# One low-part subtraction for each weight tile of a two-layer hybrid decoder

## The chip, the cores and the metric

The kernel runs on one core of one Trainium2 chip, in one launch. The metric is the device time in microseconds (us); a measurement is the median of several runs. The span named below is that of one execution taken by the profiler, from its first instruction to its last.

## The reference, cut to what matters

Two layers of a decoder on 256 tokens of width 1024, all in float32. Each layer has a token mixer, a cross attention to 256 memory tokens, and a feed-forward part: a dense SwiGLU in layer 0 and eight experts in layer 1, of which each token takes two.

```python
def swiglu(h, w_gate, w_up, w_down):
    a = jnp.einsum("bsd,df->bsf", h, w_gate)
    u = jnp.einsum("bsd,df->bsf", h, w_up)
    return jnp.einsum("bsf,fd->bsd", jax.nn.silu(a) * u, w_down)

def moe_swiglu(h, router_w, w_gate, w_up, w_down):
    ...
    for e in range(N_EXPERTS):
        y = y + gates[..., e:e + 1] * swiglu(h, w_gate[e], w_up[e], w_down[e]).astype(jnp.float32)

def reference(x, mem, ...):
    for l in range(DEPTH):
        x = x + hybrid_mixer(rmsnorm(x, norm_mix_w[l]), w_in[l], ...)
        x = x + memory_cross_attention(...)
        h = rmsnorm(x, norm_ffn_w[l])
        x = x + (swiglu(h, ...) if l % 2 == 0 else moe_swiglu(h, ...))
    return rmsnorm(x, norm_final_w)
```

The weights of the eight experts (D = 1024, width 2816) are three quarters of all bytes.

## The kernel before

**Weight tiles.** All weights come in tiles of 128 x 2048 float32 (1 MB), in the order of `weight_order`. A tile is loaded by SyncE into a staging buffer (`wst` or `wsp`). TensorE multiplies in the format fp32r; to keep float32 precision each operand is split into a high part and a low part. ScalarE makes the high part of a tile (`wh`, a rounding copy), VectorE the low part (`wl` = staged - `wh`). A product then takes three matmuls (`mm3`): high x low, low x high, high x high. When the low part is made, the staging buffer is free and SyncE, which waits for that, loads another tile.

**Buffers of the parts.** `Halves` keeps each part in two buffers of 1024 columns. Five such halves lie in a ring for `wh` and five for `wl`; in the expert stage there are seven for `wh` and six for `wl`.

**Trunk and expert stage.** Up to the dense layer and the second mixer ("trunk" below) Tile's scheduler sets the order of instructions, and `halve` splits tiles with low parts of 512 columns. The expert stage (from about 585 us) has its order written out by hand: `slot` stands for one weight tile, 264 in all, and the engines execute what it lists in that order. In slot t ScalarE makes the high halves of tile t+2, VectorE the low halves of tile t+1, TensorE the products of tile t. Small steps of the expert's own chain are posted to a later slot, at a place within it: `"act"` ahead of the first high half, `"act mid"` between the two, `"dve mid"` between the two low halves, `"pe mid"` between the two halves of the products, `"pe"` behind them.

**Long and short experts.** Experts are sorted by their number of tokens. A *long* one has up to 128 tokens: gate-up tile 12 matmuls, down tile 12. A *short* one has up to 64: its tokens' high and low parts stand side by side in the 128 columns, so a tile takes 8 matmuls, first the one with `wl`, then the one with `wh`, for each of four pieces. A chunk is 256 of the 2816 hidden channels: two gate-up tiles (`eg`) and, a few slots later, one down tile (`ed`). From the seventh long chunk on, long and short chunks come in turn, so a period of six slots is: long gate-up, long gate-up, long down (of the chunk before), short gate-up, short gate-up, short down. There are 44 chunks of each kind; the last short ones have no long one beside them.

**The chain of a chunk.** Long: ScalarE's SiLU (`es`), VectorE's product (`es`), two transposes on TensorE at the end of the next slot (`et`), ScalarE's high copy (`ehh`), VectorE's low part (`ehl`). Short: ScalarE copies the sums (`eg`), TensorE turns and adds them with eight small matmuls (`et`) in the middle of the next slot, ScalarE's SiLU, VectorE's product, then the two parts (`ehh` from both engines).

The first matmuls of a short down tile, and where they take their operands:

```python
def down(ps, h, n, k, start, stop, wh, wl):
    fs = slice(k * 1024 + n * 512, k * 1024 + (n + 1) * 512)
    for w in (wl, wh):
        nc.tensor.matmul(ps[n], h[:, k], w[:, fs], ...)
```

`products[0]` is n = 0 with k = 0 and then k = 1: two matmuls on the first half of the tile (`wl`, `wh`), then two on the second half.

Of the kernel before, what the change touches and what calls it, by code (L numbers as in the profile page):

```python
# [2 lines left out]

# [4 lines left out]
F32 = mybir.dt.float32  # L8
F32R = mybir.dt.float32r
# [3 lines left out]
ALU = mybir.AluOpType  # L13
# [3 lines left out]
P = 128  # L17
T = 256
NT = T // P
D = 1024  # L20
KD = D // P
# [12 lines left out]
LEAD = 1  # L34
CUT = (512, 1024)
STAGES = (4, 1)
HALVES = (5, {"wh": 2, "wl": 1})
WARM = (40, 72, 30, 14)
URGENT = 500
C = 64  # L40
# [43 lines left out]

class Norm:
    pass


class Halves:


    def __init__(self, *tiles):
        self.tiles = tiles

    def __getitem__(self, at):
        p, s = at
        h = s.start // 1024
        return self.tiles[h][p, s.start - h * 1024:s.stop - h * 1024]


class Trunk:
# [77 lines left out]
        self.fetched = self.nc.sync.dma_start(dst, src)  # L179
        return slot, st  # L180

    def halves(self, name):
        return Halves(*[next(self.pools[name]).tile([P, 1024], F32R, name=name) for _ in range(2)])

    def halve(self, slot, st):

        nc, tc = self.nc, self.tc
        wh, wl = self.halves("wh"), self.halves("wl")
        for q in range(2):
            s = slice(q * 1024, (q + 1) * 1024)  # L190
            self.halved = nc.scalar.activation(wh[:, s], st[:, s], AF.Copy)  # L191
            for c in range(0, 1024, self.cut):
                s = slice(q * 1024 + c, q * 1024 + c + self.cut)
                with tc.issue_after(self.hold.ins) if self.hold else nullcontext():
                    nc.vector.tensor_tensor(wl[:, s], st[:, s], wh[:, s].bitcast(F32), op=ALU.subtract)  # L195
        self.free.append(slot)
        return wh, wl
# [38 lines left out]
    def high(self, i, q):  # L236

        if i >= len(self.order) or i < self.nsplit:
            return
        if q == 0:  # L240
            self.stage()
            self.parts[i] = *self.loaded.pop(0), self.halves("wh"), self.halves("wl")
        _, st, wh, _ = self.parts[i]
        s = slice(q * 1024, (q + 1) * 1024)
        self.nc.scalar.activation(wh[:, s], st[:, s], AF.Copy)  # L245

    def low(self, i, q):
        if i not in self.parts:
            return
        slot, st, wh, wl = self.parts[i]  # L250
        s = slice(q * 1024, (q + 1) * 1024)
        with self.tc.issue_after(self.hold.ins) if self.hold else nullcontext():
            self.nc.vector.tensor_tensor(wl[:, s], st[:, s], wh[:, s].bitcast(F32), op=ALU.subtract)  # L253
        if q == 1:
            self.hold = None
            self.ready[self.order[i][0]] = wh, wl
            del self.parts[i]
            self.free.append(slot)
            self.stage()

    def slot(self, key, *products):
        t = self.nused
        assert self.order[t][0] == key, (self.order[t][0], key)
        self.now += 1
        if t + 1 < len(self.order) and t + 1 >= self.nsplit and t + 1 not in self.parts:
            self.high(t + 1, 0)
            self.high(t + 1, 1)
        self.places("act")
        self.high(t + 2, 0)
        self.low(t + 1, 0)  # L270
        self.places("dve mid", "act mid")
        self.high(t + 2, 1)
        self.low(t + 1, 1)
        w = self.ready.pop(key)
        products[0](*w)
        self.places("pe mid")
        products[1](*w)
        self.places("pe")
        self.nused += 1

    def rest(self):

        self.now += 1
        self.places("act", "dve mid", "act mid", "pe mid", "pe")


    def build(self):
# [3 lines left out]
        self.wst = pool("wst", STAGES[0])  # L291
        slot = lambda p: lambda: p.tile([P, 2048], F32, name="wst")
        self.free = [slot(self.wst)] * STAGES[0]
        self.wp = pool("wp", HALVES[0])
        self.pools = {n: repeat(self.wp) for n in ("wh", "wl")}
        self.ps = pool("ps", 8, space=PSUM)
        self.sm = pool("sm", 4)
        self.t8 = pool("t8", 6)
# [72 lines left out]
                if l % 2 == 0:  # L371
                    self.dense(l // 2, l)
        with tc.tile_pool(name="emid", bufs=1) as self.md, tc.tile_pool(name="ewkb", bufs=2) as self.wb, \
                tc.tile_pool(name="wst2", bufs=STAGES[1]) as wst2, ExitStack() as more:
            self.free += [slot(wst2)] * STAGES[1]
            for n, k in HALVES[1].items():
                p = more.enter_context(tc.tile_pool(name=f"{n}2", bufs=k))
                self.pools[n] = cycle([p] * k + [self.wp] * HALVES[0])
            self.xg = [self.big("xg", shape=(P, 2 * KD * P)) for _ in range(2)]
            self.spare()  # L380
            self.kept = self.spare()
            self.moe(0, 1)
# [818 lines left out]
    def moe(self, j, l):  # L1201
# [22 lines left out]
        def gather(lists, xg):  # L1224
# [10 lines left out]
            ps = {}  # L1235
# [35 lines left out]
            def spread(n):  # L1271

                for k in range(KD):
                    self.post(n + k, "pe", lambda k=k: products(k))
                    self.post(n + k + 1, "act mid", lambda k=k: highs(k))
                    self.post(n + k + 2, "dve mid", lambda k=k: lows(k))
                self.post(n + KD, "pe", scales)
                self.post(n + KD + 1, "dve mid", keep_scales)

            return xg, xr, steps, spread  # L1280

# [85 lines left out]
        def long(x, xr):  # L1367
            def part(pg, hf, k, wh, wl):
                c = hf * 4 + k
                fs = slice(k * 512, (k + 1) * 512)  # L1370
                self.mm3(pg, x[:, c, 0], x[:, c, 1], wh[:, fs], wl[:, fs], c == 0, c == KD - 1)

            def chain(pg):

                s = wb.tile([P, 256], F32, name="es")
                h = [wb.tile([P, 2, P], F32R, name=f"eh{p}", bufs=3) for p in "hl"]
                pt = self.psum((P, 2, P), "et")

                def turn():
                    for k in range(2):  # L1380
                        nc.tensor.transpose(pt[:, k, :], s[:, k * P:(k + 1) * P], self.ident)

                self.post(1, "act", lambda: nc.scalar.activation(s, pg[:, 0:256], AF.Silu, scale=xr))
                self.post(1, "dve mid", lambda: nc.vector.scalar_tensor_tensor(
                    s, pg[:, 256:512], xr, s, op0=ALU.mult, op1=ALU.mult))
                self.post(1, "pe", turn)
                self.post(2, "act", lambda: self.split_hi(h[0], pt))
                self.post(2, "dve mid", lambda: self.split_lo(*h, pt))
                return h

            def down(ps, h, n, k, start, stop, wh, wl):
                fs = slice(k * 1024 + n * 512, k * 1024 + (n + 1) * 512)
                self.mm3(ps[n], h[0][:, k, :], h[1][:, k, :], wh[:, fs], wl[:, fs], start, stop)

            return part, chain, down

        def short(x, xr):
# [13 lines left out]
            def chain(pg):  # L1411
# [10 lines left out]
                self.post(1, "act", lambda: nc.scalar.activation(g, pg, AF.Copy))  # L1422
                self.post(1, "pe mid", turn)
                self.post(2, "act", lambda: nc.scalar.activation(s, pt[:, 0:2, :], AF.Silu))
                self.post(2, "dve mid", lambda: nc.vector.tensor_tensor(s, s, pt[:, 2:4, :], op=ALU.mult))
                self.post(2, "act mid", lambda: self.split_hi(hs[:, :, 0, :], s))
                self.post(3, "dve mid", lambda: self.split_lo(hs[:, :, 0, :], hs[:, :, 1, :], s))
                return h

            def down(ps, h, n, k, start, stop, wh, wl):  # L1430
# [6 lines left out]
        def leave(ps, oh, gate):  # L1437
# [17 lines left out]
            rows()  # L1455
            for n in range(2):
                self.post(1 + n, "act", lambda n=n: self.split_hi(y[n][0], ps[n]))
                self.post(1 + n, "dve mid", lambda n=n: self.split_lo(*y[n], ps[n]))
            self.post(1, "dve mid", lambda: nc.vector.tensor_copy(oT, po[:, 0:T]))
            for n in range(2):  # L1460
                for i in range(NT):
                    pz = self.psum(name="ez")
                    self.post(2 + 2 * n + i, "pe", lambda pz=pz, i=i, n=n: scatter(pz, i, n))
                    self.post(3 + 2 * n + i, "dve mid", lambda pz=pz, i=i, n=n: add(pz, i, n))

        class Expert:

# [55 lines left out]
        def spread(n):  # L1523
            marks, _, rest = lists_of(n)
            for i, m in enumerate(marks):
                self.post(1 + i, "dve mid", m)
            rest(1 + len(marks))

        with self.urgent():
# [81 lines left out]
    def final_weights(self):  # L1611

        nc = self.nc
# [8 lines left out]

        for k in range(8):
            b = k // 4
            self.post(1 + k, "dve mid", lambda k=k: diagonal(k))
# [97 lines left out]
```

## Time and profile before

| what | value |
|---|---|
| median of 3 runs (lowest to highest) | 1342.04 us (1341.5 to 1342.77) |
| the profiled execution's own time | 1343.5 us |
| its span | 1341.6 us |
| mean granted TensorE clock | 0.990 |
| TensorE busy | 1293.9 us, 96% of the span |
| VectorE busy | 1162.9 us, 87% |
| ScalarE busy | 937.6 us, 70% |
| read from HBM | 365.60 MB, 273 GB/s over the span |

A busy share is an average over stages: the trunk (to about 585 us) and the expert stage have different limits. In the profile PE is TensorE's matmuls, PEld its weight loads, DVE is VectorE, ACT ScalarE, SP SyncE; L253 is line 253 of the kernel.

### The profile page before, as it was taken

What the parts mean: (1) busy time and instruction counts of PE and PEld (TensorE: products, weight loads), DVE (VectorE), ACT (ScalarE), POOL (GpSimd) and SP (SyncE); (2) the same over time, 40 slices, a digit from 0 to 9 for tenths busy, and PEclk for the clock granted to TensorE, in tenths of its full rate; (3) what the DMA queues carried; (4) which work ended last, traced back from release to release, by engine and by line L of the source; (5) the groups of instructions that cost most, each with busy time, mean ns of one, the idle gap of its engine ahead of it and who ended that gap; (6) DMA issues with size and microseconds to landing.
All of it is one profiled execution on the core that took longest, in us unless ns stands there. A gap on an engine that the chain in (4) does not pass through costs nothing.

```text
span 1341.6 us, 20691 instructions
## 1 busy us (share of the span) xinstructions
PE 1293.9 (96%) x7301; PEld 1087.7 (81%) x7301; DVE 1162.9 (87%) x2057; ACT 937.6 (70%) x1502; POOL 7.5 (1%) x30
## 2 busy tenths in 40 slices
PE   9999999999999999989999999999999999999995
PEld 8978989999999878778877787777877778777773
DVE  8998877666677988579999999999999999999997
ACT  7565575444465556558788788887888887887884
POOL 0000000000000000000000000000000000000000
PEclk9999999999999999979999999999999999999998
DMA  8423625555544424549999999999999999999990
GB/s 326 158 96 118 228 95 194 187 187 189 187 165 151 164 95 160 194 149 338 343 405 386 338 371 413 379 402 338 355 412 384 394 380 337 404 407 371 392 351 34
DMA packets 67567, 368.06 MB, mean 274 GB/s; under 512 B 5744, under 2 KB 6000, under 8 KB 38016
## 3 DMA queue, kind: packets, MB, share of 16 engines
q1 hardware_dynamic: 67136, 365.59, 72.1%
q8 instruction: 59, 0.97, 0.3%
q0 software_dynamic: 320, 1.08, 0.2%
q14 instruction: 52, 0.43, 0.1%
HBM read 365.60 MB, written 1.05 MB: 273 GB/s over the span
## 4 chain that ended last, share of the span: by engine, by line
PE 68%; DVE 20%; issue 7%; ACT 5%; DMA 0%; DVEq 0%; SPq 0%; ACTq 0%
DVE wl L253 12%; PE fm L437 5%; PE fm L439 5%; PE fm L438 5%; PE eg L437 5%; PE eg L439 5%; PE eg L438 5%; PE ed L1433 4%; PE ed L437 2%; PE ed L438 2%; PE ed L439 2%; PE et L1420 2%; PE pr L437 2%; PE pr L438 2%; PE pr L439 2%
## 5 line engine op out<-in xcount | busy, mean ns | idle before, releaser
L253 DVE TENSOR_TENSOR wl<-wst,wh 128x1024 fp32r<-128x1024 f32 x294 | 348.9, 1222 | 0.0
L245 ACT ACTIVATE wh<-wst 128x1024 fp32r<-128x1024 f32 x294 | 295.6, 1053 | 0.0
L195 DVE TENSOR_TENSOR wl<-wst,wh 128x512 fp32r<-128x512 f32 x328 | 214.8, 688 | 87.9 <-ACT wh L191 87.7
L253 DVE TENSOR_TENSOR wl<-wsp,wh 128x1024 fp32r<-128x1024 f32 x232 | 276.1, 1222 | 1.5 <-PE eg L438 1.5
L191 ACT ACTIVATE wh<-wst 128x1024 fp32r<-128x1024 f32 x164 | 171.3, 1062 | 143.7 <-PE fm L439 88.5
L245 ACT ACTIVATE wh<-wsp 128x1024 fp32r<-128x1024 f32 x232 | 234.4, 1054 | 0.3 <-PE eg L439 0.3
L437 PE MATMUL fm<-hTh,wl 128*128 128x256 f32 x736 | 207.6, 282 | 1.0 <-DVE wl L195 1.0
L438 PE MATMUL fm<-hTl,wh 128*128 128x256 f32 x736 | 206.2, 280 | 0.0
L439 PE MATMUL fm<-hTh,wh 128*128 128x256 f32 x736 | 205.9, 280 | 0.0
L1409 PE MATMUL eg<-wl,xs 128*128 128x512 f32 x352 | 143.9, 409 | 5.9 <-DVE wl L253 5.9
L437 PE MATMUL eg<-wh,xg 128*128 128x512 f32 x352 | 141.2, 401 | 0.0
L437 PEld LDWEIGHTS fm<-hTh,wl 128*128 128x128 f32 x736 | 138.3, 188 | 1.9 <-DVE wl L195 1.2
L438 PE MATMUL eg<-wl,xg 128*128 128x512 f32 x352 | 139.8, 397 | 0.0
L439 PE MATMUL eg<-wh,xg 128*128 128x512 f32 x352 | 139.8, 397 | 0.0
L438 PEld LDWEIGHTS fm<-hTl,wh 128*128 128x128 f32 x736 | 138.2, 188 | 0.8 <-issue 0.2
L439 PEld LDWEIGHTS fm<-hTh,wh 128*128 128x128 f32 x736 | 138.7, 188 | 0.0
L1409 PE MATMUL eg<-wh,xs 128*128 128x512 f32 x352 | 138.6, 394 | 0.0
L1433 PE MATMUL ed<-wl,ehh 128*128 128x512 f32 x176 | 78.1, 444 | 13.5 <-DVE wl L253 12.2
L1409 PEld LDWEIGHTS eg<-wl,xs 128*128 128x128 f32 x352 | 66.3, 188 | 23.4 <-DVE wl L253 10.7
L439 PEld LDWEIGHTS eg<-wh,xg 128*128 128x128 f32 x352 | 66.8, 190 | 15.7
L437 PEld LDWEIGHTS eg<-wh,xg 128*128 128x128 f32 x352 | 67.0, 190 | 14.8
L438 PEld LDWEIGHTS eg<-wl,xg 128*128 128x128 f32 x352 | 66.9, 190 | 14.8
(339 smaller groups left out, 2257.0 us busy)
## 6 DMA issues: line engine op xcount, KB each, us to landing
wst<-in_moe_gu_dram SPq DMA_DIRECT2D x115, 1024.0 KB, 7.0
wsp<-in_moe_gu_dram SPq DMA_DIRECT2D x61, 1024.0 KB, 6.9
wsp<-in_moe_w_down_dram SPq DMA_DIRECT2D x55, 1024.0 KB, 7.2
wst<-in_moe_w_down_dram SPq DMA_DIRECT2D x33, 1024.0 KB, 7.3
wst<-in_ffn_gu_dram SPq DMA_DIRECT2D x22, 1024.0 KB, 4.9
wst<-in_w_in_fm_dram SPq DMA_DIRECT2D x16, 1024.0 KB, 4.9
wst<-in_ffn_w_down_dram SPq DMA_DIRECT2D x11, 1024.0 KB, 4.9
wst<-in_w_in_tm_dram SPq DMA_DIRECT2D x8, 1024.0 KB, 5.0
```

Of the source, the lines that this page charges most:

```text
L191: self.halved = nc.scalar.activation(wh[:, s], st[:, s], AF.Copy)
L195: nc.vector.tensor_tensor(wl[:, s], st[:, s], wh[:, s].bitcast(F32), op=ALU.subtract)
L245: self.nc.scalar.activation(wh[:, s], st[:, s], AF.Copy)
L253: self.nc.vector.tensor_tensor(wl[:, s], st[:, s], wh[:, s].bitcast(F32), op=ALU.subtract)
L437: nc.tensor.matmul(out, ll, rh, start=start, stop=False)
L438: nc.tensor.matmul(out, lh, rl, start=False, stop=False)
L439: nc.tensor.matmul(out, lh, rh, start=False, stop=stop)
L1409: nc.tensor.matmul(pg, both[:, c], w[:, fs], start=c == 0 and w is wl, stop=c == KD - 1 and w is wh)
L1420: nc.tensor.matmul(pt[:, b, :], g[:, b * P:(b + 1) * P], comb, start=True, stop=True)
L1433: nc.tensor.matmul(ps[n], h[:, k], w[:, fs], start=start and w is wl, stop=stop and w is wh)
```

## The change

- `Halves` is gone. A part is one buffer of 128 x 2048, three for `wh` and three for `wl`, from the start to the end of the kernel. A high part is still written by two instructions of 1024 columns.
- In the expert stage `low` makes the whole low part of tile t+1 in one instruction of 2048 columns. What was posted between two low halves (`"dve mid"`) now stands behind it (`"dve"`).
- ScalarE's high part of a short chunk's hidden values goes from slot 2, `"act mid"`, to slot 3, `"act"`.
- In the trunk `halve` still works in pieces of 512 columns, but its pieces lie in whole buffers.

```diff
-HALVES = (5, {"wh": 2, "wl": 1})
+SPLITS = {"wh": 3, "wl": 3}
...
+    def parts_of(self):
+        return [self.wp.tile([P, 2048], F32R, name=n, bufs=SPLITS[n]) for n in ("wh", "wl")]
...
-            self.parts[i] = *self.loaded.pop(0), self.halves("wh"), self.halves("wl")
+            self.parts[i] = *self.loaded.pop(0), *self.parts_of()
...
-    def low(self, i, q):
+    def low(self, i):
         if i not in self.parts:
             return
-        slot, st, wh, wl = self.parts[i]
-        s = slice(q * 1024, (q + 1) * 1024)
+        slot, st, wh, wl = self.parts.pop(i)
         with self.tc.issue_after(self.hold.ins) if self.hold else nullcontext():
-            self.nc.vector.tensor_tensor(wl[:, s], st[:, s], wh[:, s].bitcast(F32), op=ALU.subtract)
-        if q == 1:
-            self.hold = None
-            self.ready[self.order[i][0]] = wh, wl
-            del self.parts[i]
-            self.free.append(slot)
-            self.stage()
+            self.nc.vector.tensor_tensor(wl, st, wh.bitcast(F32), op=ALU.subtract)
+        self.hold = None
+        self.ready[self.order[i][0]] = wh, wl
+        self.free.append(slot)
+        self.stage()
...
         self.places("act")
         self.high(t + 2, 0)
-        self.low(t + 1, 0)
-        self.places("dve mid", "act mid")
+        self.low(t + 1)
+        self.places("dve", "act mid")
         self.high(t + 2, 1)
-        self.low(t + 1, 1)
...
-                self.post(2, "act mid", lambda: self.split_hi(hs[:, :, 0, :], s))
-                self.post(3, "dve mid", lambda: self.split_lo(hs[:, :, 0, :], hs[:, :, 1, :], s))
+                self.post(3, "act", lambda: self.split_hi(hs[:, :, 0, :], s))
+                self.post(3, "dve", lambda: self.split_lo(hs[:, :, 0, :], hs[:, :, 1, :], s))
```

All other `"dve mid"` posts become `"dve"` alike. On VectorE, in a period in which long and short chunks come in turn, these rows stood before (from a long chunk's product `es` on; `wl_9111` and `wl_9112` are the halves of the first short gate-up tile, `wl_9139` and `wl_9140` of the second, `wl_9166` and `wl_9167` of the short down tile):

```order
L253 TENSOR_TENSOR wl_9111<-wst_8928,wh_9109 128x1024
L1384 SCALAR_TENSOR_TENSOR es_9132<-eg_9083,xr2_7094,es_9132 128x256
L253 TENSOR_TENSOR wl_9112<-wst_8928,wh_9110 128x1024
L253 TENSOR_TENSOR wl_9139<-wsp_6681,wh_9137 128x1024
L451 TENSOR_TENSOR ehl_9134<-et_9135,ehh_9133 128x256
L253 TENSOR_TENSOR wl_9140<-wsp_6681,wh_9138 128x1024
L253 TENSOR_TENSOR wl_9166<-wsp_6682,wh_9164 128x1024
L253 TENSOR_TENSOR wl_9167<-wsp_6682,wh_9165 128x1024
```

The same tiles of such a period on VectorE after the change (`wl_8756` is the short down tile):

```order
L242 TENSOR_TENSOR wl_8707<-wst_8545,wh_8706 128x2048
L1366 SCALAR_TENSOR_TENSOR es_8726<-eg_8683,xr2_6916,es_8726 128x256
L242 TENSOR_TENSOR wl_8732<-wsp_6511,wh_8731 128x2048
L433 TENSOR_TENSOR ehl_8728<-et_8729,ehh_8727 128x256
L242 TENSOR_TENSOR wl_8756<-wsp_6512,wh_8755 128x2048
```

The product `es` and the low part `ehl` stood between two halves of a tile and now stand between two tiles; each low instruction reads a whole `wh`. On ScalarE, at the same place before (from the second short gate-up tile `wh_9137`, `wh_9138` to the short down tile `wh_9164`, `wh_9165`):

```order
L1383 ACTIVATE es_9132<-eg_9083,xr2_7094 128x256
L245 ACTIVATE wh_9137<-wsp_6681 128x1024
L245 ACTIVATE wh_9138<-wsp_6681 128x1024
L447 ACTIVATE ehh_9133<-et_9135 128x256
L245 ACTIVATE wh_9164<-wsp_6682 128x1024
L245 ACTIVATE wh_9165<-wsp_6682 128x1024
```

And on ScalarE after the change:

```order
L1365 ACTIVATE es_8726<-eg_8683,xr2_6916 128x256
L234 ACTIVATE wh_8731<-wsp_6511 128x1024 x2
L429 ACTIVATE ehh_8727<-et_8729 128x256
L234 ACTIVATE wh_8755<-wsp_6512 128x1024 x2
```

The order is the same here, and the two high instructions of a tile now fill one buffer.

## Rows read from the trace of the kernel before

**Rows 1.** The page: busy time, share of the span and instructions of each engine.

```profile
PE 1293.9 (96%) x7301; PEld 1087.7 (81%) x7301; DVE 1162.9 (87%) x2057; ACT 937.6 (70%) x1502; POOL 7.5 (1%) x30
```

**Rows 2.** The page: the chain that ended last, by line.

```profile
DVE wl L253 12%; PE fm L437 5%; PE fm L439 5%; PE fm L438 5%; PE eg L437 5%; PE eg L439 5%; PE eg L438 5%; PE ed L1433 4%; PE ed L437 2%; PE ed L438 2%; PE ed L439 2%; PE et L1420 2%; PE pr L437 2%; PE pr L438 2%; PE pr L439 2%
```

**Rows 3.** Windows: regular periods; length, busy PE PEld DVE ACT POOL, clock, DMA, GB/s.

```profile
673.57:689.02 15.45, 15.30 (x72) 12.25 (x70) 14.90 (x17) 13.17 (x18) 0.00 (x0) 1.00 0.99 398
791.74:807.18 15.44, 15.29 (x72) 12.25 (x70) 14.90 (x17) 13.17 (x18) 0.00 (x0) 1.00 1.01 404
1187.00:1202.40 15.40, 15.24 (x72) 12.25 (x70) 15.07 (x18) 13.18 (x18) 0.00 (x0) 1.00 1.02 407
```

**Rows 4.** Timeline of PE around a short down tile: start, duration, instruction [idle before].

```profile
803.28 0.38 PE L1381 MATMUL et<-ident,es 128*128 128x128 f32 x2
803.42 0.48 PE L1409 MATMUL eg<-wl,xs 128*128 128x512 f32 x1
...
807.18 0.40 PE L1433 MATMUL ed<-wl,ehh 128*128 128x512 f32 x1
807.41 0.39 PE L1433 MATMUL ed<-wh,ehh 128*128 128x512 f32 x1
808.00 0.50 PE L1433 MATMUL ed<-wl,ehh 128*128 128x512 f32 x1 [0.20 <-DVE wl L253]
808.34 0.40 PE L1433 MATMUL ed<-wh,ehh 128*128 128x512 f32 x1
808.57 1.00 PE L1420 MATMUL et<-comb,eg 128*128 128x64 f32 x8
...
812.95 0.40 PE L439 MATMUL eg<-wh,xg 128*128 128x512 f32 x1
```

**Rows 5.** Timeline of ACT at the same place.

```profile
801.06 2.00 ACT L245 ACTIVATE wh<-wst 128x1024 fp32r<-128x1024 f32 x2
803.70 0.38 ACT L447 ACTIVATE ehh<-et 128x256 fp32r<-128x256 f32 x1 [0.64 <-PE et L1381]
803.98 3.90 ACT L245 ACTIVATE wh<-wsp 128x1024 fp32r<-128x1024 f32 x4
...
811.80 2.94 ACT L245 ACTIVATE wh<-wst 128x1024 fp32r<-128x1024 f32 x3
```

**Rows 6.** Timeline of DVE at the same place.

```profile
801.60 2.35 DVE L253 TENSOR_TENSOR wl<-wst,wh 128x1024 fp32r<-128x1024 f32 x2
804.11 0.43 DVE L451 TENSOR_TENSOR ehl<-et,ehh 128x256 fp32r<-128x256 f32 x1 [0.16 <-ACT ehh L447]
804.46 1.22 DVE L253 TENSOR_TENSOR wl<-wst,wh 128x1024 fp32r<-128x1024 f32 x1
805.59 3.49 DVE L253 TENSOR_TENSOR wl<-wsp,wh 128x1024 fp32r<-128x1024 f32 x3
```

**Rows 7.** Waits of the stage with both kinds: total us, times, longest.

```profile
PE ed L1433 <- DVE wl L253: 12.2, 36, 0.9
```

**Rows 8.** The page's groups: low parts of 1024 and of 512 columns.

```profile
L253 DVE TENSOR_TENSOR wl<-wst,wh 128x1024 fp32r<-128x1024 f32 x294 | 348.9, 1222 | 0.0
...
L195 DVE TENSOR_TENSOR wl<-wst,wh 128x512 fp32r<-128x512 f32 x328 | 214.8, 688 | 87.9 <-ACT wh L191 87.7
```

**Rows 9.** Windows: a period at an expert's end, one of short chunks alone.

```profile
838.18:855.81 17.63, 17.46 (x82) 13.85 (x80) 17.63 (x22) 14.98 (x21) 0.00 (x0) 1.00 1.00 382
...
1311.67:1318.80 7.13, 6.73 (x33) 5.17 (x32) 7.13 (x9) 6.56 (x10) 0.00 (x0) 1.00 0.00 0
```

**Rows 10.** SyncE's queue: what its weight loads waited for in the expert stage.

```profile
SPq L179 <- DVE wl L253: 547.4, 246, 5.2
```

**Rows 11.** Windows: the dense layer, the start of the expert stage, the fastest loads.

```profile
200.00:250.00 50.00, 50.00 (x380) 47.82 (x379) 34.13 (x74) 25.42 (x36) 0.00 (x0) 1.00 0.51 187
...
590.00:600.00 10.00, 8.43 (x26) 6.87 (x27) 6.65 (x35) 3.22 (x5) 0.00 (x0) 0.66 0.50 188
1150.00:1200.00 50.00, 49.44 (x228) 39.67 (x227) 48.37 (x54) 42.58 (x56) 0.00 (x0) 1.00 1.01 415
```

**Rows 12.** The page's group of the trunk's products with the low part.

```profile
L437 PE MATMUL fm<-hTh,wl 128*128 128x256 f32 x736 | 207.6, 282 | 1.0 <-DVE wl L195 1.0
```

More of the change, by code (lines that the diff above doesn't have):

```diff
@@ L1 @@
 from contextlib import ExitStack, nullcontext
-from itertools import chain, cycle, islice, repeat
+from itertools import chain, islice
 import concourse.bass as bass
@@ L86 @@
     pass
[L89 to L98, printed above, removed]
 class Trunk:
@@ L180, in load @@
         return slot, st
-    def halves(self, name):
-        return Halves(*[next(self.pools[name]).tile([P, 1024], F32R, name=name) for _ in range(2)])
+    def parts_of(self):
+        return [self.wp.tile([P, 2048], F32R, name=n, bufs=SPLITS[n]) for n in ("wh", "wl")]
     def halve(self, slot, st):
         nc, tc = self.nc, self.tc
-        wh, wl = self.halves("wh"), self.halves("wl")
+        wh, wl = self.parts_of()
         for q in range(2):
@@ L283, in rest @@
         self.now += 1
-        self.places("act", "dve mid", "act mid", "pe mid", "pe")
+        self.places("act", "dve", "act mid", "pe mid", "pe")
     def build(self):
@@ L293, in build @@
         self.free = [slot(self.wst)] * STAGES[0]
-        self.wp = pool("wp", HALVES[0])
-        self.pools = {n: repeat(self.wp) for n in ("wh", "wl")}
+        self.wp = pool("wp", 1)
         self.ps = pool("ps", 8, space=PSUM)
@@ L373, in build @@
         with tc.tile_pool(name="emid", bufs=1) as self.md, tc.tile_pool(name="ewkb", bufs=2) as self.wb, \
-                tc.tile_pool(name="wst2", bufs=STAGES[1]) as wst2, ExitStack() as more:
+                tc.tile_pool(name="wst2", bufs=STAGES[1]) as wst2:
             self.free += [slot(wst2)] * STAGES[1]
-            for n, k in HALVES[1].items():
-                p = more.enter_context(tc.tile_pool(name=f"{n}2", bufs=k))
-                self.pools[n] = cycle([p] * k + [self.wp] * HALVES[0])
             self.xg = [self.big("xg", shape=(P, 2 * KD * P)) for _ in range(2)]
@@ L1275, in spread @@
                     self.post(n + k + 1, "act mid", lambda k=k: highs(k))
-                    self.post(n + k + 2, "dve mid", lambda k=k: lows(k))
+                    self.post(n + k + 2, "dve", lambda k=k: lows(k))
                 self.post(n + KD, "pe", scales)
-                self.post(n + KD + 1, "dve mid", keep_scales)
+                self.post(n + KD + 1, "dve", keep_scales)
             return xg, xr, steps, spread
@@ L1383, in chain @@
                 self.post(1, "act", lambda: nc.scalar.activation(s, pg[:, 0:256], AF.Silu, scale=xr))
-                self.post(1, "dve mid", lambda: nc.vector.scalar_tensor_tensor(
+                self.post(1, "dve", lambda: nc.vector.scalar_tensor_tensor(
                     s, pg[:, 256:512], xr, s, op0=ALU.mult, op1=ALU.mult))
@@ L1387, in chain @@
                 self.post(2, "act", lambda: self.split_hi(h[0], pt))
-                self.post(2, "dve mid", lambda: self.split_lo(*h, pt))
+                self.post(2, "dve", lambda: self.split_lo(*h, pt))
                 return h
@@ L1424, in chain @@
                 self.post(2, "act", lambda: nc.scalar.activation(s, pt[:, 0:2, :], AF.Silu))
-                self.post(2, "dve mid", lambda: nc.vector.tensor_tensor(s, s, pt[:, 2:4, :], op=ALU.mult))
-                self.post(2, "act mid", lambda: self.split_hi(hs[:, :, 0, :], s))
-                self.post(3, "dve mid", lambda: self.split_lo(hs[:, :, 0, :], hs[:, :, 1, :], s))
+                self.post(2, "dve", lambda: nc.vector.tensor_tensor(s, s, pt[:, 2:4, :], op=ALU.mult))
+                self.post(3, "act", lambda: self.split_hi(hs[:, :, 0, :], s))
+                self.post(3, "dve", lambda: self.split_lo(hs[:, :, 0, :], hs[:, :, 1, :], s))
                 return h
@@ L1457, in leave @@
                 self.post(1 + n, "act", lambda n=n: self.split_hi(y[n][0], ps[n]))
-                self.post(1 + n, "dve mid", lambda n=n: self.split_lo(*y[n], ps[n]))
-            self.post(1, "dve mid", lambda: nc.vector.tensor_copy(oT, po[:, 0:T]))
+                self.post(1 + n, "dve", lambda n=n: self.split_lo(*y[n], ps[n]))
+            self.post(1, "dve", lambda: nc.vector.tensor_copy(oT, po[:, 0:T]))
             for n in range(2):
@@ L1463, in leave @@
                     self.post(2 + 2 * n + i, "pe", lambda pz=pz, i=i, n=n: scatter(pz, i, n))
-                    self.post(3 + 2 * n + i, "dve mid", lambda pz=pz, i=i, n=n: add(pz, i, n))
+                    self.post(3 + 2 * n + i, "dve", lambda pz=pz, i=i, n=n: add(pz, i, n))
         class Expert:
@@ L1525, in spread @@
             for i, m in enumerate(marks):
-                self.post(1 + i, "dve mid", m)
+                self.post(1 + i, "dve", m)
             rest(1 + len(marks))
@@ L1624, in final_weights @@
             b = k // 4
-            self.post(1 + k, "dve mid", lambda k=k: diagonal(k))
+            self.post(1 + k, "dve", lambda k=k: diagonal(k))
             self.post(1 + k, "pe", lambda k=k: nc.tensor.matmul(ps[k // 4][:, k % 4, :], self.ones, dg[k], start=True, stop=True))
```

## The prediction, on record before the run

> **What bounds the kernel now.** I read the page first. TensorE is busy for 96% of the span and VectorE for 87% [rows 1], and the chain that ended last names the low parts of the expert stage as its largest single line, 12% [rows 2]. So the question is which of the two sets the pace there, and that is read from the stage, not from the shares.
>
> The windows come next. From one short down tile to the next there are six tiles, and 20 such periods take 15.4 to 15.5 us each, the first, one in the middle and the last of which stand in [rows 3]. In each of them TensorE shows 15.3 us busy and VectorE 14.9, at full clock: both look like the limit.
>
> The timelines of one period show how they hang together [rows 4 to 6]. Follow the chain from the transposes at the end of the long down tile (start 803.28, end 803.66). ScalarE has waited 0.64 us for them; it copies their result (803.70) and only then makes the high parts of the short down tile. Four highs take 3.90 us from 803.98, so they are issued (3.90 - 1.05) / 3 = 0.95 apart and last 1.05, as the pair of 2.00 at 801.06 says too: the tile's first high ends at 805.03, its second at 805.98. VectorE still has half a low part to make (804.46) and begins this tile's lows at 805.59; three take 3.49 us, so 1.135 apart: they end at 806.81 and 807.94. TensorE meanwhile does the 16 matmuls of the two short gate-up tiles (803.42 to 807.18), issues the first two matmuls of the short down tile on the first half, and then stands: the third could go at 807.41 + 0.23 = 807.64 and goes at 808.00, 0.06 after the second low ended. It also takes 0.34 until the next instead of 0.23. Over the stage this wait is the 36 times of [rows 7], 0.34 us each.
>
> So in a period TensorE has about 15.45 - 0.36 - 0.11 = 15.0 us of work and one stall of 0.47, at the short down tile, where a chain TensorE - ScalarE - VectorE - TensorE comes late. Two short gate-up tiles give TensorE only 3.8 us to cover it.
>
> **The change part by part.** *One low instruction of 2048 columns.* The trace has none. From 512 to 1024 columns the low part grows from 688 to 1222 ns [rows 8], 534 per 512 columns, so 2048 take 1222 + 2 x 534 = 2290 ns. Bounds: two issue intervals, 2.27 us, and two whole durations, 2.44. I take 2.29, since growth with columns is what the two rows show. VectorE is occupied up to the next start for about 2290 - 87 = 2203 ns (a half lasts 1222 and holds the next back by 1135, 87 less), against 2270: 67 ns saved a tile.
>
> *What it waits for.* It reads the whole high part, so it can't begin before the second high has ended. At the short down tile that is 805.98 + 0.04 (as 803.66 to 803.70) = 806.02. VectorE is free by then: the tile before can begin when its second high has ended (801.06 + 2.00 + 0.04 = 803.10), is done at 805.39, and `ehl` behind it holds VectorE for 0.35 (804.11 to 804.46), to some 805.7. So the low runs from 806.02 to 808.31.
>
> *What waits for it.* TensorE's first matmul of a short tile reads `wl`, now one buffer written by one instruction: it goes at 808.31 + 0.06 = 808.37 instead of 807.18, and no two matmuls run ahead of the wait any more. Then 0.34 and three times 0.23 to the eight small `et` matmuls: 809.40, where before they stood at 808.57. The period is longer by **0.83 us**: 0.37 because the low part ends later, 0.46 for the two matmuls that ran ahead. The stall itself grows from 0.36 to 1.2 us. Nothing gives it back: the next long down tile's transposes come when TensorE has done its 15 us, so the same chain begins 0.83 later each time. The second short gate-up tile may wait about 0.1 (low done at 805.39, TensorE there at 805.34), which the longer stall behind it swallows; a long tile's first matmul reads `wh` alone, and lows that end 0.4 later meet a TensorE that is 0.8 later.
>
> *How often.* There are 44 short down tiles. 20 end the regular periods: 20 x 0.83 = 16.6. Three more stand behind the last step of a gather, with the same chain: 2.5. Twelve lie in periods where VectorE has an expert's end to add, like the 17.63 us of [rows 9] in which it is busy for 17.63: six tiles save 6 x 0.067 = 0.40 there, the two matmuls cost up to 0.46; between -0.40 and +0.46 each, I take 0. Nine are in the tail, which is short chunks alone but for two: VectorE is busy 7.13 of 7.13 us; three tiles save 0.20, the matmuls cost up to 0.46; I take +0.2 each, 1.8. Sum **20.9**.
>
> *Three whole buffers.* `wl` keeps its room. `wh` loses half a tile: the high part of a tile now waits until TensorE has left the tile three before. In the regular period one high starts earlier than that: of the three from 811.80 the second (812.75) opens a short gate-up tile, while TensorE's last matmul on the tile three before starts at 812.95 and ends at 813.35 [rows 4, 5]. It would go at 813.39, 0.64 us later, its second half end 2.0 later, and the low part at 815.39 + 0.04 + 2.29 = 817.72. TensorE has two long tiles ahead of it then, 24 matmuls of 0.23 from 813.18, so it asks at 818.7: hidden by 1 us. Cost 0 to 0.64, taken as 0.
>
> *Posts behind the low, `ehh` of a short chunk a slot later.* Their readers are TensorE's transposes at a slot's end or a down tile more slots on: 0. VectorE no longer stands with half a tile undone when `es` or `ehl` is late (0.16 in [rows 6]); already in the walk above.
>
> *Trunk.* The scheduler shifts instructions a little, since the ring holds six halves' room instead of five. TensorE is busy 50.00 of 50 us in the dense layer [rows 11] and waited for low parts for 1.0 us in all [rows 12], so at most 1 us is to be had; some transposes move by up to six matmuls of 0.23 at four places, at most 5.5 us of loss. I take 0.
>
> *Loads.* SyncE's queue waits for low parts [rows 10], not the other way; a slower stage asks for less than the 400 GB/s of [rows 3]. 0.
>
> The sum for the profiled execution is 1343.5 + 20.9 = 1364.4. It stands 1.5 above the median of the runs, so the median should come to 1342.04 + 20.9 = 1362.9, say **1363**.
>
> **The rivals.** *Faster: VectorE is the bound, and 67 ns a tile count.* For it: the largest line of the chain, and 14.9 of 15.45 us busy. 264 x 0.067 = 17.7, so 1324; it holds if the whole low part ends before TensorE asks for its first half. Against it: at the short down tile it asked at 807.18, and even the first half was only 0.37 us old.
>
> *Faster still: whole durations count.* If each low instruction cost VectorE its whole duration, one of 2290 for two of 1222 would save 154 ns a tile, 264 x 0.154 = 40.7, so 1301. Against it stand two back to back in 2.35 us, not 2.44 [rows 6]: part of the duration is overlapped already.
>
> The Trainium skill ("VectorE: DVE Perf Modes", section on the TRN2 errata) states such a rule: an SBUF operation pays a fixed latency for each instruction, so one large tile beats many small ones; its formula for a float32 `tensor_tensor` gives 2291 ns at 2048 columns. The trace agrees with the duration; with the gain only as far as the 67 ns above.
>
> *Half of it: ScalarE is not the limit.* If VectorE could begin the low part at 805.59 after all, it would end at 807.88 and `et` come 0.40 later, not 0.83: 23 x 0.40 + 1.8 = 11, so 1353. It needs the second high 0.4 us earlier; nothing moves the transposes for which ScalarE waits.
>
> *No change.* The 0.46 lost at each short down tile is met by 6 x 0.067 = 0.40 saved on VectorE, if its six lows run without a gap: 1343. Against it, the gap ahead of the low part in the walk, 0.3 us.
>
> *Buffers decide.* If the high that moves by 0.64 sets the pace, 20 x 0.64 = 12.8 come on top: 1376. It does from the point where the two long tiles hide less than that.
>
> *Clock.* TensorE was granted 0.66 in the window 590 to 600, where it stood for part of it; at the stage's end it had 1.00 with 6.73 busy of 7.13 [rows 9, 11]. If a stall of 1.2 us brought the lower level, twelve matmuls at twice 0.23 would cost 2.8 a period: 1363 + 56 = 1419.
>
> **How the numbers follow.** The forecast has 0.76, the half 0.07, the buffers 0.05, the clock 0.02, no change 0.04, faster 0.05 and faster still 0.01. The range takes in the half case and the bounds: downwards the tail and the expert ends at their low ends (-3.6 and -4.8) and the trunk's 1 us, with the half case at 1353; upwards the expert ends (+5.5), the tail (+2.3) and a low part of 2.44 instead of 2.29 (23 x 0.15 = 3.5). That is 1351 to 1374, and leaves out 0.17. A measurement of this kernel tells about 0.2% from no change; faster by more than that has 0.06, within it 0.04, slower 0.90.
>
> **What would show it.** In the changed kernel's trace: regular periods of 16.3 us; PE's wait at the first `ed` matmul of a short down tile instead of the third, some 1.2 us, put down to `wl`; low parts of 2.29 us; ahead of the short down tile's low a gap on VectorE put down to ScalarE's high; no wait of a long tile; the clock at 1.00; the expert stage beginning where it did. The forecast is wrong if the low part is much shorter than 2.29, or if that gap and the wait are not there.

## The result and the profile after

The changed kernel takes 1363.29 us (median of 4 runs, 1362.47 to 1363.73); the kernel before took 1342.40 beside it (4 runs, 1341.5 to 1343.88). The ratio is 1.0154 [1.0136, 1.0171]: slower, by 20.9 us. The profiled execution took 1363.73 us with a span of 1362.0, 20.4 more than before.

The page of the changed kernel: busy time by engine, and the chain that ended last, by line.

```profile
PE 1299.7 (95%) x7301; PEld 1088.4 (80%) x7301; DVE 1148.6 (84%) x1794; ACT 939.5 (69%) x1502; POOL 6.5 (0%) x30
...
DVE wl L242 7%; PE ed L1415 7%; PE eg L419 6%; PE eg L420 6%; PE eg L421 6%; ACT wh L234 6%; PE fm L419 5%; PE fm L420 5%; PE fm L421 5%; PE ed L419 3%; PE ed L420 3%; PE ed L421 3%; PE et L1402 3%; PE pr L419 2%; PE pr L421 2%
...
L242 DVE TENSOR_TENSOR wl<-wst,wh 128x2048 fp32r<-128x2048 f32 x147 | 335.0, 2289 | 25.6 <-ACT wh L234 25.0
```

VectorE has 263 instructions and 14.3 us of work less than in [rows 1], and the kernel is slower. In the chain the low part fell from 12% [rows 2] to 7%, and ScalarE's high part `wh`, which was not among those lines, now has 6%. That is the first sign of a low part that waits for a high part.

Windows of the changed kernel: two regular periods, the first expert's end, a later one, the start of the expert stage (length, busy PE PEld DVE ACT POOL, clock, DMA, GB/s).

```profile
676.33:692.62 16.29, 15.50 (x71) 12.16 (x71) 14.62 (x11) 13.33 (x18) 0.00 (x0) 1.00 0.98 380
797.64:813.96 16.32, 15.50 (x71) 12.19 (x71) 14.71 (x11) 13.41 (x18) 0.00 (x0) 1.00 0.99 368
...
725.24:743.33 18.09, 16.27 (x74) 12.77 (x75) 15.93 (x15) 15.17 (x20) 0.00 (x0) 1.00 0.97 374
846.59:864.16 17.57, 17.42 (x81) 13.97 (x81) 17.37 (x16) 14.48 (x20) 0.00 (x0) 1.00 0.99 363
590.00:600.00 10.00, 6.85 (x25) 5.63 (x26) 6.88 (x38) 4.16 (x7) 0.00 (x0) 0.83 0.54 204
```

A regular period has 16.3 us where it had 15.44 [rows 3]. In it VectorE does less than before (14.71 against 14.90), TensorE's work is nearly the same, and loads move 368 to 380 GB/s where they moved 398 to 407. The clock is at its full level.

Timelines of the changed kernel around the short down tile at the end of the second of these periods: PE, then ACT, then DVE (start, duration, instruction, [idle before]).

```profile
810.71 0.40 PE L1391 MATMUL eg<-wh,xs 128*128 128x512 f32 x1
811.03 0.50 PE L1391 MATMUL eg<-wl,xs 128*128 128x512 f32 x1
811.37 0.39 PE L1391 MATMUL eg<-wh,xs 128*128 128x512 f32 x1
...
812.74 0.40 PE L1391 MATMUL eg<-wh,xs 128*128 128x512 f32 x1
813.96 0.50 PE L1415 MATMUL ed<-wl,ehh 128*128 128x512 f32 x1 [0.82 <-DVE wl L242]
814.29 0.40 PE L1415 MATMUL ed<-wh,ehh 128*128 128x512 f32 x1
...
814.99 1.00 PE L1402 MATMUL et<-comb,eg 128*128 128x64 f32 x8
```

```profile
806.65 2.00 ACT L234 ACTIVATE wh<-wst 128x1024 fp32r<-128x1024 f32 x2
809.30 0.39 ACT L429 ACTIVATE ehh<-et 128x256 fp32r<-128x256 f32 x1 [0.65 <-PE et L1363]
809.58 3.89 ACT L234 ACTIVATE wh<-wsp 128x1024 fp32r<-128x1024 f32 x4
```

```profile
808.68 2.29 DVE L242 TENSOR_TENSOR wl<-wst,wh 128x2048 fp32r<-128x2048 f32 x1 [0.41 <-ACT wh L234]
810.89 0.42 DVE L433 TENSOR_TENSOR ehl<-et,ehh 128x256 fp32r<-128x256 f32 x1
811.61 4.49 DVE L242 TENSOR_TENSOR wl<-wsp,wh 128x2048 fp32r<-128x2048 f32 x2 [0.30 <-ACT wh L234]
```

Read them as one chain, against [rows 4 to 6]. ScalarE waits 0.65 for the transposes, copies (809.30), and makes four highs, 0.947 apart; the second ends at 809.58 + 0.947 + 1.05 = 811.58. VectorE has stood for 0.30 and begins the whole low part at 811.61. It ends at 813.90, and TensorE's first `ed` matmul goes 0.06 later. That matmul could have gone at 812.74 + 0.23 = 812.97, so the stall is 0.99. None of the tile's matmuls ran ahead of it. Another 0.2 us stands at the second short gate-up tile, whose first matmul also waits for a whole low part: it goes 0.32 behind the one ahead of it (811.03), and the next another 0.34 later, where 0.23 is the usual distance.

Waits of the changed kernel in the stage with both kinds of chunks and its tail (total us, times, longest).

```profile
DVE wl L242 <- ACT wh L234: 48.2, 118, 1.2
...
PE ed L1415 <- DVE wl L242: 26.0, 34, 1.1
ACT wh L234 <- PE ed L1415: 24.0, 38, 0.7
```

TensorE's wait for low parts of the down tiles is 26.0 us in 34 pieces, where [rows 7] had 12.2 in 36. VectorE's wait for highs stands ahead of it.

### The profile page after: what moved, and what is told of

Same layout as the page of the kernel before. It is cut to its first block, busy times and chain, and to the rows that moved or that the text cites. A ratio compares the mean times of both kernels' runs of the same rounds, so it can differ in the third digit from the quotient of the medians.

```text
span 1362.0 us, 20151 instructions
## 1 busy us (share of the span) xinstructions
PE 1299.7 (95%) x7301; PEld 1088.4 (80%) x7301; DVE 1148.6 (84%) x1794; ACT 939.5 (69%) x1502; POOL 6.5 (0%) x30
## 3 DMA queue, kind: packets, MB, share of 16 engines
HBM read 365.60 MB, written 1.05 MB: 269 GB/s over the span
## 4 chain that ended last, share of the span: by engine, by line
PE 74%; DVE 13%; ACT 8%; issue 3%; DMA 1%; SPq 0%; ACTq 0%; DVEq 0%
DVE wl L242 7%; PE ed L1415 7%; PE eg L419 6%; PE eg L420 6%; PE eg L421 6%; ACT wh L234 6%; PE fm L419 5%; PE fm L420 5%; PE fm L421 5%; PE ed L419 3%; PE ed L420 3%; PE ed L421 3%; PE et L1402 3%; PE pr L419 2%; PE pr L421 2%
## 5 line engine op out<-in xcount | busy, mean ns | idle before, releaser
L242 DVE TENSOR_TENSOR wl<-wst,wh 128x2048 fp32r<-128x2048 f32 x147 | 335.0, 2289 | 25.6 <-ACT wh L234 25.0
L242 DVE TENSOR_TENSOR wl<-wsp,wh 128x2048 fp32r<-128x2048 f32 x116 | 265.0, 2290 | 31.3 <-ACT wh L234 31.3
L1391 PEld LDWEIGHTS eg<-wl,xs 128*128 128x128 f32 x352 | 66.2, 188 | 24.9 <-DVE wl L242 12.9
L420 PEld LDWEIGHTS eg<-wl,xg 128*128 128x128 f32 x352 | 66.6, 189 | 16.2 <-DVE wl L242 1.0
```

The lines of the kernel that those rows point to most:

```text
L242: self.nc.vector.tensor_tensor(wl, st, wh.bitcast(F32), op=ALU.subtract)
L420: nc.tensor.matmul(out, lh, rl, start=False, stop=False)
L1391: nc.tensor.matmul(pg, both[:, c], w[:, fs], start=c == 0 and w is wl, stop=c == KD - 1 and w is wh)
```

## The experiments

All but the last start from the changed kernel. The expert stage is cut into 44 pieces at the first matmul of each short down tile. The first piece holds all slots ahead of the first short down tile (81 us before); 19 of the others are regular periods. Lengths minus those of before, from one profiled execution of each kernel, in us:

| kernel | first piece | 19 regular | 3 gather ends | 12 expert ends | 9 tail | stage |
|---|---|---|---|---|---|---|
| the change | +1.4 | +16.3 | +2.8 | -3.4 | +1.9 | +18.9 |
| two halves, posts behind both | 0.0 | -0.1 | -0.9 | -4.2 | -0.8 | -6.0 |
| two halves, posts between | -0.4 | +0.7 | -0.1 | +0.4 | +0.1 | +0.6 |
| two halves at short down tiles alone | +1.5 | +1.8 | -0.7 | -4.9 | +0.7 | -1.6 |
| high parts first at short down tiles | +0.7 | +7.9 | -0.4 | -4.0 | +1.1 | +5.3 |
| hidden copy behind the highs | +3.0 | +7.0 | +0.1 | -3.9 | +1.9 | +8.0 |
| two halves and hidden copy between | +0.9 | -4.4 | -0.9 | -3.6 | -0.6 | -8.7 |
| four whole buffers for `wh` | +2.3 | +16.2 | +2.8 | -3.4 | +1.1 | +18.9 |
| before, hidden copy between | +0.7 | -4.7 | -0.2 | -1.4 | -0.3 | -5.9 |

The theory was that of the prediction: the whole low part comes late at the short down tile, for two reasons (0.37 and 0.46 us), in a chain that starts at the long tile's transposes. The rivals were VectorE's own work, the whole buffers, and the places of the posts.

**Two halves, posts behind both.** Whole buffers and the new places of the posts stay; the low part alone is undone.

```diff
-            self.nc.vector.tensor_tensor(wl, st, wh.bitcast(F32), op=ALU.subtract)
+            for q in range(2):
+                s = slice(q * 1024, (q + 1) * 1024)
+                self.nc.vector.tensor_tensor(wl[:, s], st[:, s], wh[:, s].bitcast(F32), op=ALU.subtract)
```

> The changed kernel, with the low part of each tile of the expert stage in two instructions of 1024 columns again, one behind the other, in the whole buffers and with the posts behind both. Theory (a whole low part is late at each short down tile): the stall goes back to the third matmul of a short down tile, the regular period from 16.3 to 15.4 us or a little less, since VectorE no longer stands between two halves; 23 x 0.83 + 1.8 + 5 for the expert ends, so 1336 to 1342. Rival 1 (three whole buffers of the high part make it slow): no change, 1363. Rival 2 (the posts behind the low part make it slow): no change, 1363.

Measured: 1334.69 us, 0.994 [0.9922, 0.9959] of before, and under the range expected. The window of a regular period and that of the first expert's end:

```profile
787.78:803.23 15.45, 15.31 (x71) 12.25 (x70) 14.93 (x17) 13.30 (x18) 0.00 (x0) 1.00 1.00 395
717.04:734.41 17.37, 16.56 (x75) 12.45 (x73) 15.32 (x21) 15.23 (x21) 0.00 (x0) 1.00 1.00 386
```

The regular period is as long as before, so one instruction for two is what costs. Buffers and posts cost nothing there. The stall, though, is not at the third matmul, where the theory put it. PE at the short down tile that ends the period, and a wait of the stage with both kinds:

```profile
803.47 0.39 PE L1417 MATMUL ed<-wh,ehh 128*128 128x512 f32 x1
803.70 0.39 PE L1417 MATMUL ed<-wl,ehh 128*128 128x512 f32 x1
803.92 0.40 PE L1417 MATMUL ed<-wh,ehh 128*128 128x512 f32 x1
804.46 0.77 PE L1404 MATMUL et<-comb,eg 128*128 128x64 f32 x5
```

```profile
PEld et L1404 <- ACT eg L1406: 15.3, 27, 0.7
```

The third matmul (803.70) goes 0.23 behind the second, without a wait. TensorE stands at `et` instead, which comes 0.54 behind the last matmul and 0.06 after ScalarE's copy `eg` (803.82, 0.58 long) has ended. That copy stands behind four highs that start at 800.03, so the chain through ScalarE still sets the period, by another of its links. In 17 of the 19 regular periods the wait is there; in two it is at the third matmul.

The kernel as a whole is faster than before, and the table puts most of that in the expert ends.

**Two halves, posts between.** As above, with the posts back between the halves. In the expert stage only the buffers, and the slot of the short chunk's `ehh`, then differ from before.

```diff
...
         self.high(t + 2, 0)
-        self.low(t + 1)
+        self.low(t + 1, 0)
         self.places("dve", "act mid")
         self.high(t + 2, 1)
+        self.low(t + 1, 1)
```

> As the run with halves behind each other, but with the posts between the two halves, as in the kernel before: what is left of the change are the whole buffers and the later high part of a short chunk. Theory: as the kernel before, 1342, plus at most the 1.4 us by which the expert stage began later; period 15.45. Rival 1 (buffers): 1363. Rival 2 (posts): 1342, and the run with posts behind would be slow.

Measured: 1341.28 us, 0.9991 [0.9982, 1.0001]: no difference. The same two windows:

```profile
787.29:802.79 15.50, 15.31 (x71) 12.24 (x70) 14.93 (x17) 13.30 (x18) 0.00 (x0) 1.00 1.02 418
715.39:734.33 18.94, 16.75 (x76) 12.60 (x74) 16.30 (x22) 15.23 (x21) 0.00 (x0) 1.00 0.94 356
```

Before, this expert's end took about as long as here:

```profile
720.01:738.84 18.83, 16.70 (x75) 12.61 (x74) 16.26 (x22) 15.08 (x21) 0.00 (x0) 1.00 0.94 356
```

So the posts alone are worth 18.94 - 17.37 = 1.57 us at this expert's end, 4.6 over the twelve pieces of expert ends, and 1341.28 - 1334.69 = 6.6 for the kernel. DVE's timeline there, with the posts between the halves and then behind both, shows how:

```profile
723.28 1.22 DVE L243 TENSOR_TENSOR wl<-wsp,wh 128x1024 fp32r<-128x1024 f32 x1
724.90 0.48 DVE L1370 SCALAR_TENSOR_TENSOR es<-eg,xr,es 128x256 f32<-128x256 f32 x1 [0.40 <-ACT es L1369]
727.63 0.29 DVE L1495 TENSOR_SCALAR oh<-twice,sorted 128x128 fp32r<-128x128 bf16 x1 [2.24 <-PE eo L1431]
727.83 1.22 DVE L243 TENSOR_TENSOR wl<-wsp,wh 128x1024 fp32r<-128x1024 f32 x1
```

```profile
724.41 2.35 DVE L244 TENSOR_TENSOR wl<-wsp,wh 128x1024 fp32r<-128x1024 f32 x2
726.68 0.48 DVE L1368 SCALAR_TENSOR_TENSOR es<-eg,xr,es 128x256 f32<-128x256 f32 x1
729.21 0.29 DVE L1493 TENSOR_SCALAR oh<-twice,sorted 128x128 fp32r<-128x128 bf16 x1 [2.05 <-PE eo L1429]
```

Both wait over 2 us for TensorE's `eo`. In the first the second half of a tile stands behind that wait, and the lows behind it come late; in the second the tile is finished. With the posts between, TensorE then waits in this window, and with the posts behind it has no such wait:

```profile
PE eg L1395 <- DVE wl L243: 2.0, 2, 1.4
```

`oh` waits so at three of the twelve pieces, and these three gain 5.1 us. The piece behind each loses part of it again, 2.3 us together; the other six gain 1.7. What happens in those nine was not traced.

Taken in this order, the stage's 18.9 us of the table are +24.9 for the whole low part (18.9 + 6.0), -6.6 for the posts, and +0.6 for the buffers and the slot of `ehh`.

**Two halves at short down tiles alone.** The 44 tiles on which the prediction rests are undone; the other 219 stay whole.

```diff
+            name, _, n = self.order[i][0][:3]
+            cut = 1024 if name == "dn" and n // NFC % 2 else 2048
+            for c in range(0, 2048, cut):
+                s = slice(c, c + cut)
+                self.nc.vector.tensor_tensor(wl[:, s], st[:, s], wh[:, s].bitcast(F32), op=ALU.subtract)
```

> The changed kernel, with two low instructions for the 44 short down tiles alone and one for the 220 others. Theory: nearly all of the loss is back, 1340 to 1344, period 15.5, for the stall stands at these tiles only. Rival (a later whole low costs at every tile): 44 of 264 parts of 21 us come back, 1360.

Measured: 1339.34 us, 0.9977 [0.9965, 0.999]. One sixth of the tiles gives back the whole 21 us and 3 more, part of it in the expert ends. In the 19 regular periods it is 14.5 of 16.3 us; the other 1.8 goes only when the other tiles are halved too, as the first experiment shows. The period of the rows above is 15.55 here:

```profile
792.33:807.88 15.55, 15.52 (x71) 12.17 (x70) 14.69 (x12) 13.40 (x18) 0.00 (x0) 1.00 1.00 377
```

**High parts first at short down tiles.** The low part stays whole and late; the two matmuls with `wh`, which need ScalarE alone, run ahead of the two with `wl`. Only the order of a sum changes.

```diff
-                fs = slice(k * 1024 + n * 512, k * 1024 + (n + 1) * 512)
-                for w in (wl, wh):
-                    nc.tensor.matmul(ps[n], h[:, k], w[:, fs], ...)
+                if k == 0:
+                    return
+                for w in (wh, wl):
+                    for j in range(2):
+                        fs = slice(j * 1024 + n * 512, j * 1024 + (n + 1) * 512)
+                        nc.tensor.matmul(ps[n], h[:, j], w[:, fs], ...)
```

> The changed kernel, with the four matmuls of each half of a short down tile's products in another order: the two with the high part ahead of the two with the low part (the sum is the same, its order is not). Theory: two matmuls run ahead of the wait again and 0.46 of the 0.83 us come back, period 15.85; some 30 of the 44 tiles, so 1349. Rival (it is the high part for which TensorE really waits): they can't run ahead, 1363.

Measured: 1347.45 us, 1.004 [1.0027, 1.0053]. Window of the regular period, and PE at its end:

```profile
790.71:806.57 15.86, 15.50 (x71) 12.16 (x70) 14.62 (x11) 13.42 (x18) 0.00 (x0) 1.00 0.99 381
```

```profile
790.71 0.62 PE L1418 MATMUL ed<-wh,ehh 128*128 128x512 f32 x2
791.69 0.74 PE L1418 MATMUL ed<-wl,ehh 128*128 128x512 f32 x2 [0.36 <-DVE wl L242]
```

16.32 - 15.86 = 0.46: the two matmuls that run ahead are worth just what the prediction gave them. The low part is as late as in the changed kernel: from the start of `ehh` (787.03) to the first matmul with `wl` it is 4.66 us.

**Hidden copy behind the highs.** The long chunk's `ehh`, the copy that waits for the transposes, goes behind the short down tile's highs, and its low part a slot later. The highs then no longer wait for the transposes.

```diff
         self.high(t + 2, 1)
+        self.places("act end")
...
-                self.post(2, "act", lambda: self.split_hi(h[0], pt))
-                self.post(2, "dve", lambda: self.split_lo(*h, pt))
+                self.post(2, "act end", lambda: self.split_hi(h[0], pt))
+                self.post(3, "dve", lambda: self.split_lo(*h, pt))
```

> The changed kernel (whole low parts) with ScalarE's high copy of a long chunk's hidden values, which waits for the transposes, behind the two high parts of its slot instead of ahead of them, and VectorE's low part of these values a slot later. Theory (the chain goes through ScalarE's wait for the transposes): the high parts of the short down tile no longer begin 0.7 us after the transposes, and its low part ends earlier; what holds it next is the tile three before (three buffers), so not all comes back: period 15.8, 1350. Rival (VectorE's longer instruction is late by itself): no change, 1363.

Measured: 1351.92 us, 1.0064 [1.0041, 1.0088]. The regular period, and ACT ahead of its end:

```profile
795.52:811.34 15.82, 15.50 (x71) 12.18 (x71) 14.70 (x11) 13.34 (x18) 0.00 (x0) 1.00 1.01 393
```

```profile
806.95 2.01 ACT L234 ACTIVATE wh<-wsp 128x1024 fp32r<-128x1024 f32 x2 [0.42 <-PE ed L422]
808.86 0.36 ACT L430 ACTIVATE ehh<-et 128x256 fp32r<-128x256 f32 x1
```

0.50 us of the period came back, so the chain does run through ScalarE's wait for the transposes. The rest doesn't: the short down tile's first high now waits 0.42 for TensorE to leave the tile three before. Here the rival of the buffers holds, once the wait ahead of it is gone; that is read from this wait, and was not tried with a fourth buffer.

**Two halves and hidden copy between.** The first experiment, with the long `ehh` between the two highs (`"act mid"`) and its low part in slot 3.

```diff
-                self.post(2, "act", lambda: self.split_hi(h[0], pt))
-                self.post(2, "dve", lambda: self.split_lo(*h, pt))
+                self.post(2, "act mid", lambda: self.split_hi(h[0], pt))
+                self.post(3, "dve", lambda: self.split_lo(*h, pt))
```

> Two low instructions for each tile, posts behind both, whole buffers, and the high copy of a long chunk's hidden values between the two high parts of its slot (its low part a slot later). Theory: the stall at the short down tile is gone altogether and TensorE's own 15.0 us and 0.2 set the period: 15.2, another 4 to 5 us under the run with halves behind each other, 1330. Rival (VectorE's 14.9 us busy are the limit): as that run, 1335.

Measured: 1333.62 us, 0.9933 [0.9908, 0.9959]. The expected 1330 was not reached. The regular period is 15.25 with TensorE busy in all of it, as expected; but an expert's end loses part of that (21.46 us for the piece behind the first end, 20.69 in the first experiment). The intervals of the two overlap: which is the faster isn't settled. Both beat the kernel before.

```profile
788.38:803.63 15.25, 15.25 (x71) 12.24 (x70) 15.01 (x17) 13.31 (x18) 0.00 (x0) 1.00 1.01 392
```

**Four whole buffers for `wh`.** The rival of the buffers, by itself; a staging buffer is given up for the room.

```diff
-STAGES = (4, 1)
-SPLITS = {"wh": 3, "wl": 3}
+STAGES = (3, 1)
+SPLITS = {"wh": 4, "wl": 3}
```

> The changed kernel with four whole buffers for the high part instead of three, and, to make room, one staging buffer fewer. Theory (buffers don't decide): period 16.3 as before, 1362 to 1363. Rival (the high part waits for TensorE to leave the tile three before, and that sets the pace): 10 us or more less, 1350. If the missing staging buffer tells, it is slower and the run says nothing of the high part's buffers.

Measured: 1368.44 us, 1.0189 [1.0165, 1.0213]. The period doesn't move:

```profile
802.26:818.58 16.32, 15.50 (x70) 12.19 (x71) 14.61 (x11) 13.30 (x18) 0.00 (x0) 1.00 0.99 384
```

ScalarE's 38 waits for `ed` of the changed kernel (24.0 us) are not among its waits any more, so they were hidden there. The expectation said that a slower run tells nothing of the buffers, and it is slower. But the time lost is not in the stage (751.3 us in both): the profiled execution's stage began 3.7 us later. So for the stage the run does tell. That the missing staging buffer is the reason for the later start was only argued.

**Before, hidden copy between.** The kernel before with the same two posts moved, and nothing else.

```diff
-                self.post(2, "act", lambda: self.split_hi(h[0], pt))
-                self.post(2, "dve mid", lambda: self.split_lo(*h, pt))
+                self.post(2, "act mid", lambda: self.split_hi(h[0], pt))
+                self.post(3, "dve mid", lambda: self.split_lo(*h, pt))
```

> The kernel before (halves, posts between them) with nothing changed but the high copy of a long chunk's hidden values between the two high parts of its slot, and its low part a slot later. Theory: the stall of 0.47 at the short down tile in the kernel before has the same source, so the period goes from 15.45 to 15.2 and the time to 1335 to 1337. Rival (VectorE is the limit there): no change, 1342.

Measured: 1336.5 us, 0.9947 [0.9928, 0.9966]. The regular period is 15.14, TensorE busy in all of it, and the 19 are 0.25 shorter in the mean. The stall of 0.36 us that [rows 4] show at the short down tile was this chain's too: 0.10 us of it is left (the third matmul goes 0.33 behind the second, at 809.93).

```profile
794.23:809.37 15.14, 15.14 (x72) 12.26 (x70) 14.80 (x17) 13.20 (x17) 0.00 (x0) 1.00 1.00 400
```

## Why the prediction was right

The forecast, 1363 us, is the time measured, and its mechanism is shown. That it came out to the microsecond is luck, though: one term was 3.4 us too high, and four others were 2.9 too low together.

**The late low part: right.** From the start of `ehh` to the first `ed` matmul the walk had 808.37 - 803.70 = 4.67 us; it is 813.96 - 809.30 = 4.66. From there to `et` it had 1.03, and it is 1.03. Low parts take 2289 and 2290 ns for 2290 foreseen. Undoing 44 low parts gives back nearly all of it in the regular periods; letting two matmuls run ahead gives 0.46. The other part, 0.37, was not undone by itself; it is what is left of the whole, 0.86 a period, but for 0.03. The stall at the first `ed` matmul is 0.99 where the prediction had some 1.2: the 0.2 at the second short gate-up tile, foreseen as about 0.1, comes ahead of it in the same chain and makes the period no longer.

**Regular periods: 17.7 for 16.6.** The trace of before has 19 such periods, not 20; the twentieth of these short down tiles ends the first piece. The 19 cost 16.3, so 0.86 each for 0.83. The 0.03 lies between the short chunk's `et` and the next long tile's transposes (10.21 us for 10.18 in the mean) and was not traced further. The first piece costs 1.4 for 0.83; with four buffers, and the stage's instructions as they are here, it costs 2.3, so this figure isn't a steady one. **Gather ends** 2.8 for 2.5, **tail** 1.9 for 1.8.

**Expert ends: -3.4 for 0, the term that failed.** The sum weighed 67 ns a tile against the matmuls that no longer run ahead, and costed "Posts behind the low" at nothing because their readers come late enough. It looked at who reads a post. It should have asked what a post that waits holds up behind it: between two halves, the wait of `oh` for `eo` kept half a tile from TensorE. The posts alone give -4.6 there (the second experiment against the first); with whole lows -3.4 is left. The three pieces with this wait have -2.8 of it and the three behind them -0.6. The other six, to which the 17.63 us of [rows 9] belong, have 0.0 together: for the kind of piece that the sum looked at, the term held. The bounds of the term (-4.8 to +5.5) took in the whole.

**Trunk: 0, not separable.** The stage began 1.4 us later than before (593.8 against 592.4), and this made the sum come out: 17.7 + 2.8 - 3.4 + 1.9 + 1.4 = 20.4. In the six experiments that have the same code up to there and as many buffers it began between 588.2 and 593.1, and with the code of before at 592.4 and 595.7. So the 1.4 can't be put down to the change, and that it helps the sum is chance.

**Buffers: 0, right as long as the low part is late.** The wait of 0.7 at most is there, 38 times, and a fourth buffer that removes it changes no period. The experiment that took the transposes out of the chain shows the point from which it counts.

**The rivals.** VectorE does not set the pace: it has less to do and the period is longer. That one low instruction saves 67 ns on VectorE was right (two of them in 4.49 us start 4.49 - 2.29 = 2.20 apart, where two halves took 2.27), and the time goes into a longer wait. The Trainium skill ("VectorE: DVE Perf Modes", section on the TRN2 errata) says that one large tile pays the fixed latency once. The measured 2289 to 2290 ns agree with the 2291 of its formula. Yet with a saving of 67 ns for each of 263 tiles the kernel still lost 20.9 us, since TensorE waited for a whole tile where the first half had been enough. The clock stayed at 1.00 in the regular periods.

## What to carry to other kernels

Before two instructions become one, see who waits for the first half and who delivers the second. Here the longer one started 0.03 us after its last input and released TensorE only 0.06 after its end. What it saves on its engine counts only if that engine sets the pace there. A small step that may wait belongs behind a finished tile, not in the middle of one. And when a chain is late, look for the one copy in it that waits: moving it alone brought the kernel before to 0.9947 of its time.

## What was not expected

The posts, a part of the change that the sum took at nothing, gain 6.6 us where the whole change costs 20.9: with them behind two halves the kernel is faster than it was before. And with the low part in halves again, TensorE's wait did not go back to where it had been, but to the next link of the same chain.

A TensorE that stands for 1.0 us in each 16.3 us keeps the granted clock at 1.00 from 656 to 1310 us of the changed kernel, as the forecast had it. Lower values stand elsewhere, as where the stage starts: 0.66 and 0.83 in the windows 590 to 600 of before [rows 11] and after.
